# Forget gates computed inside the values' product, their block sums through DRAM, in a streaming-encoder layer

## The chip, the cores and the metric

The kernel runs on one core of a Trainium2 chip. The metric is device time in microseconds (us), from one execution to the next of the same program. TensorE (PE) does the matrix products, VectorE (DVE) and ScalarE (ACT) the elementwise work, GpSimd (POOL) a little of it, and SyncE (SP) issues every transfer.

## What is computed

One post-norm layer over a sequence of 1024 rows of width 1024: a token mixer with two branches (forgetting attention and a gated linear recurrence), then a SwiGLU feed-forward layer. The part that the change touches is the forget gate of the attention, one column of `f_a` for each of the 8 heads:

```python
proj = x @ w_in
q_a, k_a, v_a, f_a, q_b, f_b, i_b, g_b, gate_a, gate_b = jnp.split(proj, IN_SPLITS, axis=-1)
log_fa = jax.nn.log_sigmoid(f_a + b_f)              # (B, S, 8)
y_a = fox_attention(q_a, k_a, v_a, log_fa)
...
F = jnp.cumsum(log_f, axis=1).transpose(0, 2, 1)    # along the sequence
s = einsum(q_i, kh) * scale + fq_i[..., None] - F[:, :, None, :]
p = softmax(where(causal, s, -inf)); o = p @ vh
```

So no score can be finished before the running sum F of the gates' logarithms is there for its head.

## The kernel before

The whole layer is one program. Each matrix product is made with operands that are split in a high and a low part (`split`: ACT rounds to the high part, DVE subtracts it for the low part) and three matmuls for each pair. The values `v_a` and `i_b` are one product of x (1024 by 1024) with a weight (1024 by 1024), made by a recursion with seven products of half size instead of eight, p1 to p7. With x cut in quarters (x11 and x12 are the first 512 rows, x21 and x22 the last), its operands are x11 (p1), x12 (p2), x22 (p4), the sum x21 + x22 (p5), and three other sums (p6, p7, p3). The products run in the order p1, p2, p4, p5, p6, p7, p3, 48 matmuls of 512 columns each. Their names in the trace: `Tvp5h` and `Tvp5l` are the high and low part of p5's weight, `vs2`, `vs3` and `vs4` the operands of p6, p7 and p3, `vx` and `vy` the results (four PSUM banks each), `x_r` the loaded last rows of x, `vbm` the second half of the values on its way to `vb_d` in DRAM.

Then `qk_first` makes queries and keys of the first two heads with the same recursion (`qk_s`, `qk_pt`, seven products of 12 matmuls). In its middle, before queries are copied out, it calls `forget_gates`:

1. 32 matmuls, x against 8 columns of weights (`wf`, high and low part beside each other in 40 columns), give `fo` in two halves of 512 rows, and ACT and DVE add high and low results into `fs`.
2. Eight transfers turn this into one tile `f4` of 64 partitions (8 blocks of 128 rows times 8 heads), called `f` in the trace.
3. Some twelve small steps on ACT and DVE make the logarithms and a running sum along each block of 128 rows.
4. A matmul with a constant matrix `before` gives each block the sum of the blocks ahead of it, and two DVE steps add it.
5. The result goes to `nf_d` in DRAM.

`attention` handles the heads in pairs. For each head it loads `nf_d` broadcast to 128 partitions into a quarter of `box1` (`box` in the trace, 512 KB), POOL adds the causal mask to a copy of it in two steps, and for each block of 128 queries PE makes the scores `s`, DVE adds the bias and takes the maximum (`soft`), ACT takes the exponential, POOL scales, and PE transposes (`pt`) and multiplies with the values (`pv`).

All calls are first written down by a planner and then issued engine by engine in the order that its costs give (`Plan.schedule`): a call goes where its engine is free first in the plan, and among those the one that was written down earliest. The plan prices a transfer at its bytes over 358 GB/s, plus 1.95 us until it lands, and 60 ns of SP's time. The products of eight of the later gates (`gps`, weights `wg`) are written down with a rank that lets them fill what PE has free. Each engine then runs its own list strictly in order, and SP issues all transfers in one list into one queue. Tiles come out of pools with a fixed number of buffers: `box1` is in the pool of `vbm`, which has one buffer, so the first transfer into `box1` waits until all eight transfers of `vbm` to `vb_d` have been done. In the same way the weights of the second head pair (`wq_r`, 512 KB) take the buffer of a high part of `vs2`.

Of the kernel before, what the change touches and what calls it, by code (L numbers as in the profile page):

```python
# [7 lines left out]
F32 = mybir.dt.float32  # L8
# [274 lines left out]
def trunk(ctx: ExitStack, tc, a: dict, out: bass.AP):  # L283
# [52 lines left out]
    def split(hi, lo, src):  # L336
        act.copy(hi, src)
        dve.tensor_sub(lo, src, f(hi))
# [149 lines left out]

    vops["p5"] = A21
    for c in range(4):  # L490
        s1 = half("gt", f"vs1r{c}")
        dve.tensor_add(s1, a21[c], a22[c])
        split(vops["p5"][0][c], vops["p5"][1][c], s1)
    product("p5", T1, vy, True)
# [5 lines left out]
    for c in range(4):  # L500
        s3 = half("gt", f"vs3r{c}")
        dve.tensor_sub(s3, f(A11[0][c]), a21[c])
# [3 lines left out]
        split(vops["p7"][0][c], vops["p7"][1][c], s3)  # L506
    product("p6", T2, vx, True)
# [7 lines left out]
    bf = const("bf", [NT * HA, 1])  # L515
    before = const("before", [NT * HA, NT * HA + 2])
# [19 lines left out]


    wfr = const("w_f", [P, KC, HA])
    nf_d = dram.tile([NT, HA, P], F32, name="nf_d")

    def forget_gates():

        LO = 32
        wf = half("gt", "wf", F32R)[:, :KC * (LO + HA)].rearrange("p (c h) -> p c h", h=LO + HA)
        same = wfr[:, :, None, :].to_broadcast([P, KC, LO // HA - 1, HA])
        dve.tensor_sub(wf[:, :, HA:LO].rearrange("p c (a h) -> p c a h", h=HA), same, same)
        split(wf[:, :, :HA], wf[:, :, LO:], wfr)
        fs = box1[:HA, 3, :]
        for hf in range(2):
            fo = bank("h", f"fo{hf}")[:LO + HA]  # L550
            for c in range(KC):
                h, l = X(c)
                mm(fo, wf[:, c], h[:, hs(hf)], start=c == 0, stop=c == KC - 1)
                mm(fo[:HA], wf[:, c, :HA], l[:, hs(hf)], start=False, stop=c == KC - 1, skip_group_check=True)
            act.copy(fs[:, hs(hf)], fo[LO:])
            dve.tensor_add(fs[:, hs(hf)], fo[:HA], fs[:, hs(hf)])


        BH = NT * HA
        f4 = half("gt", "f4")[:BH]  # L560
        fps = f4[:, blk(1)]
        for t in range(NT):
            sync.dma_start(fps[t * HA:(t + 1) * HA], fs[:, blk(t)])
        fz, fa, fe, fu = (f4[:, blk(i)] for i in (0, 1, 2, 3))
        act.activation(fe, fps, AF.Abs, bias=bf, scale=1.0)
# [1029 lines left out]
```

## Time and profile before

| | us |
|---|---|
| median of 3 runs (lowest, highest) | 1486.25 (1485.85, 1486.31) |
| the profiled execution's own time | 1485.11 |
| its span, first to last instruction | 1483.3 |
| PE busy in the span | 1452.9 |

The page gives busy time by engine and the span in 40 slices. The views of the trace used below are: busy time by stage, with the clock that TensorE was granted (1.00 is 2.4 GHz, 0.50 is 1.2 GHz) and what the transfers moved; the timeline of one engine, where a bracket at the end of a row gives the idle time just before it and what ended it; and the rows of one tile. A row's start is counted from the first instruction of the span.

### The profile page before, as it was taken

What the parts mean: (1) busy time and instruction counts of PE and PEld (TensorE: products, weight loads), DVE (VectorE), ACT (ScalarE), POOL (GpSimd) and SP (SyncE); (2) the same over time, 40 slices, a digit from 0 to 9 for tenths busy, and PEclk for the clock granted to TensorE, in tenths of its full rate; (3) what the DMA queues carried; (4) which work ended last, traced back from release to release, by engine and by line L of the source; (5) the groups of instructions that cost most, each with busy time, mean ns of one, the idle gap of its engine ahead of it and who ended that gap; (6) DMA issues with size and microseconds to landing.
All of it is one profiled execution on the core that took longest, in us unless ns stands there. A gap on an engine that the chain in (4) does not pass through costs nothing.

```text
span 1483.3 us, 19094 instructions
## 1 busy us (share of the span) xinstructions
PE 1452.9 (98%) x6807; PEld 1193.0 (80%) x6807; DVE 1105.8 (75%) x2087; ACT 676.8 (46%) x1163; POOL 97.0 (7%) x116
## 2 busy tenths in 40 slices
PE   9997999999999999999999899999999999999998
PEld 6866888778887887788888778888888888888887
DVE  7976686776887889744838898666666666698597
ACT  6536576587576575334511343333332333434330
POOL 0003232220001000000001000000000000000000
PEclk9998999999999999999999999999999999999999
DMA  7033212221112234446720303333333335977741
GB/s 262 11 105 78 66 52 69 61 77 37 56 44 71 75 125 157 149 142 217 262 61 1 114 22 127 97 96 103 105 106 107 107 107 174 330 269 227 259 160 57
DMA packets 82208, 175.97 MB, mean 119 GB/s; under 512 B 8128, under 2 KB 21312, under 8 KB 82112
## 3 DMA queue, kind: packets, MB, share of 16 engines
q1 hardware_dynamic: 82112, 174.74, 36.2%
q8 instruction: 54, 0.88, 0.2%
q14 instruction: 42, 0.34, 0.1%
HBM read 135.58 MB, written 39.09 MB: 118 GB/s over the span
## 4 chain that ended last, share of the span: by engine, by line
PE 87%; DVE 6%; DMA 4%; issue 1%; ACT 1%; SPq 1%; POOL 1%; DVEq 0%; POOLq 0%; ACTq 0%
PE p L279 14%; PE fb L279 11%; PE fc L279 8%; PE fa L279 8%; PE bps L279 7%; PE pps L279 6%; PE o L279 6%; PE gs L279 5%; PE gps L279 3%; PE pv L279 2%; PE kps L279 2%; PE vx L279 2%; PE s L279 2%; PE pt L279 2%; PE qps L279 2%; PE vy L279 1%
## 5 line engine op out<-in xcount | busy, mean ns | idle before, releaser
L279 PE MATMUL p<-dp 128*128 128x512 f32 (+1 forms) x957 | 210.0, 382 | 0.0
L279 PEld LDWEIGHTS p<-dp 128*128 128x128 f32 x957 | 175.4, 188 | 34.7
L279 PE MATMUL fc<-xs,Tp 128*128 128x512 f32 x528 | 127.1, 389 | 0.0
L279 PE MATMUL fb<-xs,Tp 128*128 128x512 f32 x528 | 126.7, 389 | 0.0
L279 PE MATMUL fa<-x,Tp 128*128 128x512 f32 x480 | 115.7, 389 | 0.3 <-DVE u L279 0.3
L279 PEld LDWEIGHTS fc<-xs,Tp 128*128 128x128 f32 x528 | 99.1, 188 | 20.7 <-ACT xs L279 0.2
L279 PEld LDWEIGHTS fb<-xs,Tp 128*128 128x128 f32 x528 | 99.2, 188 | 20.6
L279 ACT CAST Tp<-t 128x512 fp32r<-128x512 f32 x88 | 54.3, 620 | 116.5 <-PE fc L279 71.9
L279 DVE TENSOR_TENSOR Tp<-t,Tp 128x512 fp32r<-128x512 f32 x88 | 60.6, 690 | 60.5 <-ACT Tp L279 60.1
L279 PEld LDWEIGHTS fa<-x,Tp 128*128 128x128 f32 x480 | 90.1, 188 | 19.3 <-ACT p L279 0.7
L279 ACT CAST dp<-dap 128x1024 fp32r<-128x1024 f32 (+1 forms) x42 | 41.1, 982 | 95.6 <-PE p L279 48.8
L279 PE MATMUL bps<-xl,wb_h 128*128 128x512 f32 x192 | 76.0, 396 | 0.0
L279 PE MATMUL bps<-xh,wb_h 128*128 128x512 f32 x192 | 76.0, 396 | 0.0
L279 PE MATMUL bps<-xh,wb_l 128*128 128x512 f32 x192 | 75.7, 396 | 0.0
L279 POOL TENSOR_TENSOR norm<-norm,mhalf 128x1 f32<-128x1 f32 x16 | 14.6, 914 | 882.5 <-DVE norm L279 882.5
L279 DVE TENSOR_TENSOR tl<-pt,th 128x512 fp32r<-128x512 f32 (+1 forms) x96 | 50.6, 552 | 16.5 <-ACT th L279 15.9
L279 ACT ACTIVATE p<-p,soft 128x128 f32<-128x128 f32 (+3 forms) x64 | 49.5, 775 | 22.4 <-DVE soft L279 22.0
L279 DVE TENSOR_TENSOR dp<-dap,dp 128x1024 fp32r<-128x1024 f32 (+1 forms) x42 | 47.4, 1129 | 14.9 <-ACT dp L279 14.9
L279 PE MATMUL fb<-x,Tp 128*128 128x512 f32 x240 | 57.7, 389 | 0.0
L279 POOL TENSOR_SCALAR p<-p,soft 128x128 f32<-128x128 f32 (+3 forms) x64 | 47.5, 750 | 110.8 <-DVE soft L279 97.7
L279 ACT CAST th<-pt 128x512 fp32r<-128x512 f32 (+1 forms) x96 | 43.1, 477 | 23.6 <-PE pt L279 22.2
L279 ACT CAST Tp<-wg_r 128x512 fp32r<-128x512 f32 x40 | 24.9, 623 | 62.0 <-PE fb L279 32.2
(512 smaller groups left out, 3523.4 us busy)
## 6 DMA issues: line engine op xcount, KB each, us to landing
dbp<-in_w_fo SPq DMA_DIRECT2D x45, 512.0 KB
dap<-a_d SPq DMA_DIRECT2D x35, 512.0 KB
a_d<-ar SPq DMA_DIRECT2D x42, 256.0 KB
wu_r<-in_w_ff SPq DMA_DIRECT2D x20, 512.0 KB
wg_r<-in_w_ff SPq DMA_DIRECT2D x20, 512.0 KB
a_d<-as SPq DMA_DIRECT2D x33, 256.0 KB
wg_r<-in_w_g SPq DMA_DIRECT2D x16, 512.0 KB
sg<-gate_d SPq DMA_DIRECT2D x32, 256.0 KB
```

Source lines behind the costliest of these rows:

```text
L279: getattr(q.engine, method)(*args, **kw)
```

## The change

The function `forget_gates` moves up into the values' products, between the sums for p5 and the product p5. It multiplies operands that are there already. For the first half of the rows these are x11 and x12 with the weights w1 and w2, as before. For the second half they are x21 + x22 and x22, with w1 and w2 - w1, which gives x21 w1 + x22 w2. The differences stand behind the weights in `wfx` (12 instead of 8 groups of columns). The results go into two of the banks `vx`, which p4 has left.

What was eight transfers between tiles is now two to DRAM (`f_d`) and one back. The matmul for the sums of the blocks is replaced: the last column of the running sums goes to DRAM (`b_d`, 64 numbers), eight transfers bring it back (8 partitions of 8 numbers each), and DVE multiplies by a mask and adds along the row. The four tiles `vs3r` are gone: x21's raw copy is overwritten with the difference, and loaded again from DRAM afterwards for `qk_first`.

```diff
--- before.py
+++ after.py
@@ -486,11 +486,73 @@
     for t in range(4):
         act.copy(va[:, 4 + t, :], vx[t])
 
+
+    nf_d = dram.tile([NT, HA, P], F32, name="nf_d")
+
+    def forget_gates():
+
+        LO, NC = 32, KC + 4
+        wfx = keep([P, NC, HA], "wfx")
+        sync.dma_start(wfx[:, :KC], a["w_f"])
+        dve.tensor_sub(wfx[:, KC:], wfx[:, 4:KC], wfx[:, :4])
+        wf = half("gt", "wf", F32R)[:, :NC * (LO + HA)].rearrange("p (c h) -> p c h", h=LO + HA)
+        same = wfx[:, :, None, :].to_broadcast([P, NC, LO // HA - 1, HA])
+        dve.tensor_sub(wf[:, :, HA:LO].rearrange("p c (a h) -> p c a h", h=HA), same, same)
+        split(wf[:, :, :HA], wf[:, :, LO:], wfx)
+        f_d = dram.tile([NT, HA, P], F32, name="f_d")
+        for hf, ops in enumerate(((A11, A12), (vops["p5"], A22))):
+            fo = vx[1 + hf][:LO + HA]
+            for c in range(KC):
+                h, l = (x[c % 4] for x in ops[c // 4])
+                w = wf[:, c + 4 * (hf and c > 3)]
+                mm(fo, w, h, start=c == 0, stop=c == KC - 1)
+                mm(fo[:HA], w[:, :HA], l, start=False, stop=c == KC - 1, skip_group_check=True)
+            fs = half("gt", f"fs{hf}")[:HA]
+            act.copy(fs, fo[LO:])
+            dve.tensor_add(fs, fo[:HA], fs)
+            sync.dma_start(f_d[4 * hf:4 * hf + 4].rearrange("t h p -> h t p"), fs.rearrange("h (t p) -> h t p", p=P))
+
+
+        BH = NT * HA
+        f4 = half("gt", "f4")[:BH]
+        fz, fa, fe, fu = (f4[:, blk(i)] for i in range(4))
+        sync.dma_start(fa, f_d.rearrange("t h p -> (t h) p"))
+        act.activation(fe, fa, AF.Abs, bias=bf, scale=1.0)
+        dve.tensor_scalar(fa, fa, bf, 0.0, op0=ALU.add, op1=ALU.min)
+        act.activation(fe, fe, AF.Exp, scale=-1.0)
+        dve.tensor_scalar(fu, fe, 1.0, None, op0=ALU.add)
+        act.activation(fz, fu, AF.Ln)
+        dve.tensor_scalar(fu, fu, -1.0, None, op0=ALU.add)
+        dve.tensor_sub(fe, fe, fu)
+        act.activation(fu, fz, AF.Exp, scale=-1.0)
+        dve.tensor_mul(fe, fe, fu)
+        dve.tensor_add(fz, fz, fe)
+        nf = fe
+        dve.tensor_tensor_scan(nf, fz, fa, 0.0, op0=ALU.add, op1=ALU.subtract)
+
+
+        b_d = dram.tile([NT, HA], F32, name="b_d")
+        sync.dma_start(b_d.rearrange("t h -> (t h)").unsqueeze(1), nf[:, P - 1:P])
+        dve.tensor_sub(fz, fz, fa)
+        bs = fa[:, :NT]
+        for t in range(NT):
+            sync.dma_start(bs[t * HA:(t + 1) * HA], b_d.rearrange("t h -> h t"))
+        dve.tensor_mul(bs, bs, before[:, :NT])
+        base = fu[:, :1]
+        dve.tensor_reduce(base, bs, axis=mybir.AxisListType.X, op=ALU.add)
+        dve.tensor_scalar(fz, fz, before[:, NT + 1:NT + 2], base, op0=ALU.mult, op1=ALU.add)
+        dve.scalar_tensor_tensor(nf, nf, before[:, NT:NT + 1], fz, op0=ALU.mult, op1=ALU.add)
+        sync.dma_start(nf_d.rearrange("t h p -> (t h) p"), nf)
+
+    bf = const("bf", [NT * HA, 1])
+    before = const("before", [NT * HA, NT + 2])
+
     vops["p5"] = A21
     for c in range(4):
         s1 = half("gt", f"vs1r{c}")
         dve.tensor_add(s1, a21[c], a22[c])
         split(vops["p5"][0][c], vops["p5"][1][c], s1)
+    forget_gates()
     product("p5", T1, vy, True)
     vbm = take("m", [NT, NB], "vbm")
     for t in range(4):
@@ -498,12 +560,13 @@
     vops["p6"] = operand4(("wr0", "wr1", "pf", "pf"), "vs2")
     vops["p7"] = operand4(("qk", "qk", "pf", "pf"), "vs3")
     for c in range(4):
-        s3 = half("gt", f"vs3r{c}")
-        dve.tensor_sub(s3, f(A11[0][c]), a21[c])
+        s3 = a21[c]
+        dve.tensor_sub(s3, f(A11[0][c]), s3)
         dve.tensor_add(s3, s3, f(A11[1][c]))
         dve.tensor_sub(a22[c], a22[c], s3)
         split(vops["p6"][0][c], vops["p6"][1][c], a22[c])
         split(vops["p7"][0][c], vops["p7"][1][c], s3)
+        sync.dma_start(s3, a["xT"][c][:, hs(1)])
     product("p6", T2, vx, True)
     for t in range(4):
         dve.tensor_add(vbm[:, t, :], vx[t], p1v[t])
@@ -512,8 +575,6 @@
     product("p7", T3, vx, False)
     ident = const("ident", [P, P])
     causal = const("causal", [P, 2, P], BF16, "mask")
-    bf = const("bf", [NT * HA, 1])
-    before = const("before", [NT * HA, NT * HA + 2])
 
     vops["p3"] = operand4(("kb", "kb", "qk", "qk"), "vs4")
     for c in range(4):
@@ -535,55 +596,6 @@
         sync.dma_start(vb_d[t], vbm[:, t, :])
 
 
-    wfr = const("w_f", [P, KC, HA])
-    nf_d = dram.tile([NT, HA, P], F32, name="nf_d")
-
-    def forget_gates():
-
...
-        fs = box1[:HA, 3, :]
-        for hf in range(2):
-            fo = bank("h", f"fo{hf}")[:LO + HA]
-            for c in range(KC):
-                h, l = X(c)
-                mm(fo, wf[:, c], h[:, hs(hf)], start=c == 0, stop=c == KC - 1)
-                mm(fo[:HA], wf[:, c, :HA], l[:, hs(hf)], start=False, stop=c == KC - 1, skip_group_check=True)
-            act.copy(fs[:, hs(hf)], fo[LO:])
-            dve.tensor_add(fs[:, hs(hf)], fo[:HA], fs[:, hs(hf)])
-
-
-        BH = NT * HA
-        f4 = half("gt", "f4")[:BH]
-        fps = f4[:, blk(1)]
-        for t in range(NT):
-            sync.dma_start(fps[t * HA:(t + 1) * HA], fs[:, blk(t)])
-        fz, fa, fe, fu = (f4[:, blk(i)] for i in (0, 1, 2, 3))
...
-        base = bank("h", "fbase")[:BH, :1]
-        mm(base, before[:, :BH], nf[:, P - 1:P], start=True, stop=True)
-        dve.tensor_sub(fz, fz, fa)
-        dve.tensor_scalar(fz, fz, before[:, BH + 1:BH + 2], base, op0=ALU.mult, op1=ALU.add)
-        dve.scalar_tensor_tensor(nf, nf, before[:, BH:BH + 1], fz, op0=ALU.mult, op1=ALU.add)
-        sync.dma_start(nf_d.rearrange("t h p -> (t h) p"), nf)
-
-
     ya_d = dram.tile([4, P, S], F32, name="ya_d")
 
     def qk_tiles(p):
@@ -641,7 +653,6 @@
         act.copy(p1, oa)
         mul("p2", b21, oa, False)
         dve.tensor_sub(t2, b22, b12)
-        forget_gates()
         qk_heads(0, 0, oa, *tiles)
         mul("p6", t2, ob, True)
         dve.tensor_add(u2, ob, p1)
@@ -1514,11 +1525,11 @@
         nw = 64 // L
         for c in range(2):
             lmask[:, c, nw - 1:2 * nw - 1] = (s[:, None] // (2 * L) == np.arange(nw)) & (s[:, None] // L % 2 == c)
-    bh = np.arange(NT * HA)
-    t, h = bh // HA, bh % HA
-    before = np.zeros((NT * HA, NT * HA + 2), np.float32)
-    before[:, :-2] = (h[:, None] == h) & ((t[:, None] < t) | (t[:, None] == t) & (t % 2 == 1))
-    before[:, -2], before[:, -1] = 1 - 2 * (t % 2), t % 2
+    t = np.arange(NT * HA)[:, None] // HA
+    b = np.arange(NT)
+    before = np.zeros((NT * HA, NT + 2), np.float32)
+    before[:, :-2] = (b < t) | (b == t) & (t % 2 == 1)
+    before[:, -2:] = np.concatenate([1 - 2 * (t % 2), t % 2], axis=1)
     return {"before": before, "ident": ident, "causal": causal, "once": once,
             "lmask": lmask}
 
```

How the lists of the engines read at three places follows; in each, the first block is the kernel before and the second the changed one.

SP, from the transfers of `vbm` to the loads that the first head pair waits for (`f_213<-box_179` and `f_128<-b_d` are the two forms of the small loads, `box<-nf_d` the bias of one head each, the `wq_r` behind `vb_d` the weights of the second head pair; those of the first pair, `wq_r` and `wk_r`, show in the second block only):

```order
L279 DMA vb_d<-vbm 128x512 x8
L279 DMA f_213<-box_179 8x128 x8
L279 DMA wq_r<-in_w_qk 128x1024
L279 DMA wg_0_r<-in_w_g 128x1024
L279 DMA nf_d<-f_213 64x128
L279 DMA box_179<-nf_d 128x8x128 x2
L279 DMA wg_1_r<-in_w_g 128x1024
L279 DMA wk_r<-in_w_qk 128x1024
```

```order
L279 DMA f_128<-b_d 8x8x1 x8
L279 DMA nf_d<-f_128 64x128
L279 DMA wq_r<-in_w_qk 128x1024
L279 DMA wk_r<-in_w_qk 128x1024
L279 DMA vb_d<-vbm 128x512 x8
L279 DMA box_181<-nf_d 128x8x128 x2
L279 DMA wq_r<-in_w_qk 128x1024
L279 DMA wg_0_r<-in_w_g 128x1024
```

Before, the second pair's `wq_r` stands ahead of the two bias loads; now it stands behind them, and they follow the transfers of `vbm` at once.

ACT, ahead of the copies of the keys (`k`, `kl`) that the first scores read:

```order
L279 COPY box_179<-fo_211 8x512
L279 COPY box_179<-fo_212 8x512
L279 ACTIVATE f_213<-f_213,bf 64x128
L279 ACTIVATE f_213<-f_213 64x128 x2
L279 CAST wq_h_368<-wq_r 128x512
L279 ACTIVATE f_213<-f_213 64x128
L279 CAST k_0_0_200<-qk_u_193 64x512 x2
L279 CAST k_0_1_201<-qk_u_193 64x512 x2
```

```order
L279 ACTIVATE q_0_1_201<-qk_s 64x512
L279 CAST wq_h_365<-wq_r 128x512
L279 CAST k_0_0_202<-qk_u_195 64x512 x2
L279 CAST k_0_1_203<-qk_u_195 64x512
L279 CAST kl_0_204<-kl_0_204 64x512
L279 CAST k_0_1_203<-qk_u_195 64x512
L279 CAST kl_1_205<-kl_1_205 64x512
L279 CAST k_0_0_202<-qk_p_196 64x512 x2
```

The steps on `f` are gone from there, and the cast of `wq_r` stands ahead of the first copy of the keys in both.

DVE, at the end of p7's operands and the beginning of p3's (`vs4l`):

```order
L279 TENSOR_TENSOR Tvp7l_156<-b_1_81,Tvp7h_152 128x512
L279 TENSOR_TENSOR x_r<-xh_67,x_r 128x512
L279 TENSOR_TENSOR vbm<-vx_74,p1v_106 128x512
L279 TENSOR_TENSOR x_r<-x_r,xl_69 128x512
L279 TENSOR_TENSOR x_r<-xh_67,x_r 128x512 x2
L279 TENSOR_TENSOR vs4l_163<-x_r,vs4h_161 128x512
L279 TENSOR_TENSOR x_r<-x_r,xl_69 128x512 x2
L279 TENSOR_TENSOR x_r<-xh_67,x_r 128x512
L279 TENSOR_TENSOR vs4l_163<-x_r,vs4h_161 128x512
```

```order
L279 TENSOR_TENSOR x_r<-xh_67,x_r 128x512
L279 TENSOR_TENSOR vbm<-vx_72,p1v_105 128x512
L279 TENSOR_TENSOR x_r<-x_r,xl_69 128x512
L279 TENSOR_TENSOR x_r<-xh_67,x_r 128x512
L279 TENSOR_TENSOR f_128<-f_128,before 64x8
L279 TENSOR_TENSOR x_r<-xh_67,x_r 128x512
L279 TENSOR_REDUCE f_128<-f_128 64x1
L279 TENSOR_TENSOR vbm<-vx_73,p1v_106 128x512
L279 TENSOR_SCALAR f_128<-f_128,before 64x128
L279 TENSOR_TENSOR vs4l_167<-x_r,vs4h_165 128x512
L279 SCALAR_TENSOR_TENSOR f_128<-f_128,before 64x128
```

The last steps of the gates' chain stand between the steps for `vs4`; the first of them reads what the eight small loads bring.

## Rows read from the trace of the kernel before

**Rows 1.** The page, busy time of the engines: us, share, instructions

```profile
PE 1452.9 (98%) x6807; PEld 1193.0 (80%) x6807; DVE 1105.8 (75%) x2087; ACT 676.8 (46%) x1163; POOL 97.0 (7%) x116
```

**Rows 2.** Busy time by stage: stretch, length, engines, clock, transfers' share, GB/s

```profile
33.00:100.00 67.00, 67.00 (x295) 52.38 (x294) 64.55 (x112) 33.03 (x58) 0.00 (x0) 1.00 0.14 49
...
122.00:128.00 6.00, 0.98 (x5) 0.48 (x3) 0.32 (x3) 0.00 (x0) 1.50 (x2) 0.82 0.69 122
128.00:136.00 8.00, 6.33 (x21) 4.83 (x22) 3.80 (x25) 2.98 (x9) 3.89 (x6) 0.71 0.45 169
```

**Rows 3.** PE's timeline around the attention's start: start, us, engine, line, operation

```profile
108.77 0.39 PE L279 MATMUL qk_pt<-vs3h,Tqkp7l 128*128 128x512 f32 x1
110.86 0.50 PE L279 MATMUL s<-k,q 128*128 128x128 f32 x2 [1.71 <-ACT k L279]
...
122.59 0.39 PE L279 MATMUL gps<-xh,wg_l 128*128 128x512 f32 x1
128.13 0.77 PE L279 MATMUL s<-k,q 128*128 128x512 f32 x1 [5.14 <-DVE soft L279]
...
134.44 0.33 PE L279 MATMUL pt<-ident,p 128*128 128x128 f32 x1 [1.55 <-POOL p L279]
```

**Rows 4.** The gates' chain on DVE, SP and POOL: timelines of these engines

```profile
111.31 0.41 DVE L279 TENSOR_TENSOR_SCAN f<-f 64x128 f32<-64x128 f32 x1
114.02 0.51 SPq L279 DMA_DIRECT2D nf_d<-f  x1
117.11 1.02 SPq L279 DMA_DIRECT2D box<-nf_d  x2
126.50 2.27 POOL L279 TENSOR_TENSOR box<-box,causal 128x512 f32<-128x512 f32 x2 [126.06 <-DMA box<-nf_d]
132.87 1.15 POOL L279 TENSOR_TENSOR box<-box,causal 128x512 f32<-128x512 f32 x1 [4.11 <-DMA box<-nf_d]
```

**Rows 5.** The gates' tile `fo`: its matmuls with a high part

```profile
L279 PE MATMUL fo<-xh,wf x16: 387/397/403, 90.6 to 100.3; 128*40 128x512 f32 x16
```

**Rows 6.** PE's first matmuls of p7 and p3, DVE's last steps for p3

```profile
63.41 0.39 PE L279 MATMUL vx<-Tvp7h,vs3h 128*128 128x512 f32 x1
74.29 0.39 PE L279 MATMUL vy<-Tvp3h,vs4h 128*128 128x512 f32 x1
72.09 1.30 DVE L279 TENSOR_TENSOR Tvp3l<-b,Tvp3h 128x512 fp32r<-128x512 f32 x2
73.29 1.29 DVE L279 TENSOR_TENSOR p1v<-vx,p1v 128x512 f32<-128x512 f32 x2
```

**Rows 7.** Small transfers and what waited for them: SP's and ACT's timelines

```profile
102.31 2.64 SPq L279 DMA_DIRECT2D f<-box  x4
106.21 0.40 ACT L279 ACTIVATE f<-f,bf 64x128 f32<-64x128 f32 x1 [4.64 <-DMA f<-box]
24.42 3.76 SPq L279 DMA_DIRECT2D x_r<-in_xT  x8
71.05 1.28 ACT L278 ACT_TABLE_LOAD   x1
```

**Rows 8.** The second pair's weights on SP, then ACT's copies behind their cast

```profile
105.06 0.37 SPq L279 DMA_DIRECT2D wq_r<-in_w_qk  x1
108.83 0.62 ACT L279 CAST wq_h<-wq_r 128x512 fp32r<-128x512 f32 x1 [1.28 <-DMA wq_r<-in_w_qk]
116.99 0.61 ACT L279 CAST kl<-kl 64x512 fp32r<-64x512 f32 x1
118.30 1.29 ACT L279 ACTIVATE q<-qk_p 64x512 fp32r<-64x512 f32 x2
```

**Rows 9.** The load issued behind the bias loads (SP); transfers by stage

```profile
118.99 2.82 SPq L279 DMA_DIRECT2D wg_r<-in_w_g  x1
118.00:125.00 7.00, 4.98 (x22) 3.78 (x21) 3.02 (x5) 2.12 (x4) 0.00 (x0) 1.00 0.79 72
126.00:133.00 7.00, 4.76 (x12) 3.55 (x12) 2.54 (x18) 2.98 (x9) 2.39 (x3) 0.52 0.47 167
```

More of the change, by code (lines that the diff above doesn't have):

```diff
@@ L535, in trunk @@
         sync.dma_start(vb_d[t], vbm[:, t, :])
-    wfr = const("w_f", [P, KC, HA])
-    nf_d = dram.tile([NT, HA, P], F32, name="nf_d")
-    def forget_gates():
[L543 to L547, printed above, removed]
-        fs = box1[:HA, 3, :]
-        for hf in range(2):
-            fo = bank("h", f"fo{hf}")[:LO + HA]
-            for c in range(KC):
-                h, l = X(c)
-                mm(fo, wf[:, c], h[:, hs(hf)], start=c == 0, stop=c == KC - 1)
-                mm(fo[:HA], wf[:, c, :HA], l[:, hs(hf)], start=False, stop=c == KC - 1, skip_group_check=True)
-            act.copy(fs[:, hs(hf)], fo[LO:])
-            dve.tensor_add(fs[:, hs(hf)], fo[:HA], fs[:, hs(hf)])
-        BH = NT * HA
-        f4 = half("gt", "f4")[:BH]
-        fps = f4[:, blk(1)]
-        for t in range(NT):
-            sync.dma_start(fps[t * HA:(t + 1) * HA], fs[:, blk(t)])
-        fz, fa, fe, fu = (f4[:, blk(i)] for i in (0, 1, 2, 3))
-        act.activation(fe, fps, AF.Abs, bias=bf, scale=1.0)
-        dve.tensor_scalar(fa, fps, bf, 0.0, op0=ALU.add, op1=ALU.min)
-        act.activation(fe, fe, AF.Exp, scale=-1.0)
-        dve.tensor_scalar(fu, fe, 1.0, None, op0=ALU.add)
-        act.activation(fz, fu, AF.Ln)
-        dve.tensor_scalar(fu, fu, -1.0, None, op0=ALU.add)
-        dve.tensor_sub(fe, fe, fu)
-        act.activation(fu, fz, AF.Exp, scale=-1.0)
-        dve.tensor_mul(fe, fe, fu)
-        dve.tensor_add(fz, fz, fe)
-        nf = fe
-        dve.tensor_tensor_scan(nf, fz, fa, 0.0, op0=ALU.add, op1=ALU.subtract)
-        base = bank("h", "fbase")[:BH, :1]
-        mm(base, before[:, :BH], nf[:, P - 1:P], start=True, stop=True)
-        dve.tensor_sub(fz, fz, fa)
-        dve.tensor_scalar(fz, fz, before[:, BH + 1:BH + 2], base, op0=ALU.mult, op1=ALU.add)
-        dve.scalar_tensor_tensor(nf, nf, before[:, BH:BH + 1], fz, op0=ALU.mult, op1=ALU.add)
-        sync.dma_start(nf_d.rearrange("t h p -> (t h) p"), nf)
     ya_d = dram.tile([4, P, S], F32, name="ya_d")
```

## The prediction

> **What bounds the kernel.** I read the page first: PE is busy for 1452.9 us of a span of 1483.3 [rows 1], so some 30 us are open to any change that leaves PE's work alone, as this one does. Busy time by stage then tells where. From 33 to 100 us PE has no idle time at all, and DVE is busy for 64.55 of these 67 us [rows 2]: the values' stage is full on both engines, and that is where the work goes. From 122 to 128 us PE does 0.98 us of work, and from 128 to 136 it runs at a mean clock of 0.71 [rows 2]: that is the hole. PE's timeline names its parts: 1.71 us of waiting for the copies of the keys before the first score, 5.14 us for a bias step on DVE, and 1.55 us for POOL before the first transpose [rows 3]. The last two come from the gates' chain, and the other engines show it: the running sum ends at 111.7, its write is issued at 114.02, the two bias loads follow at 117.11, and POOL can start on the first head at 126.50 and on the second at 132.87 [rows 4]. So the hole is a chain that starts too late, and its longest links are the bias loads: 126.5 - 117.1 = 9.4 us for the first head, 15.8 for both.
>
> **The matmuls** move as they are: 32 before and after. Of 512 columns each, they cost what p7's do: 48 from 63.41 to 74.29, 0.227 us each [rows 6]; the tile of the gates shows the same 0.39 us from start to end as any of these [rows 5]. So PE comes 32 x 0.227 = 7.3 us later to p3 and the same amount sooner out of the queries' products: zero in sum. For the small matmul over the blocks I carry nothing.
>
> **DVE's steps** move too. A step of 512 columns takes 0.60 us (two from 72.09 to 73.29 [rows 6]); ahead of p3's last operand there come two such steps and some 15 small ones, none above the 0.41 us of the running sum [rows 4] and most near half of it, together about 5 us. Before, DVE finishes p3's operands at 73.3 and PE wants the last of them ten matmuls behind 74.29, at 76.5 [rows 6]: 3.2 us to spare. With PE 7.3 us later, DVE may still stand and wait for 3.2 + 7.3 - 5 = 5.5 us before PE has to wait with it. Covered, if the next term stays below that.
>
> **The chain's transfers.** PE ends the gates' matmuls near 50.4 (p5 starts two products of 10.9 before 63.41, with six matmuls ahead of the 32), and ACT and DVE add 1.3. A transfer that the next one waits for takes 3.1 us on a write to DRAM (114.02 to 117.11 [rows 4]) and about 1.9 on a small load: four of them go out in 2.64 us from 102.31, so the last near 104.3, and ACT starts at 106.21 [rows 7]. The tile `f4` is there at 51.8 + 3.1 + 1.9 = 56.8. From there to the end of the running sum it was 106.21 to 111.72 before [rows 4, 7], 5.5 us; the load of the activation table, 1.28 us and hidden before [rows 7], now stands in it: 63.6. Then the write of the block sums, 3.1, and eight loads. Their spacing is 0.47 us by the large loads and 0.66 by the small ones [rows 7], so the last goes out 3.3 to 4.6 us after the first, and 1.9 more: 71.9 to 73.2. I take 73.2, from the small ones. DVE comes to the step that reads them after eight steps of 0.60 and two small ones, near 69. It stands for about 4 us, and everything on its list stands behind it. That is below 5.5, so p3 costs nothing, with some 1.3 us in hand.
>
> **The bias loads.** They need the buffer of `vbm`, whose last transfer waits for DVE: from 73.2 the list has 35 steps of 512 columns and 1.5 us of small ones, 22.5 us, so 95.7. A transfer to DRAM is worth 1.9 to 3.1; at 2.5 the bias loads go out at 98.2, 19 us sooner than at 117.11. By the same 9.4 and 15.8 us they are there at 107.6 and 114.0. The first scores are not due before 110, so the waits of 5.14 and 1.55 us and the slow stretch behind them are gone as far as the bias is their cause. That alone would be worth some 8 us.
>
> **What is late next.** The weights `wq_r` of the second head pair. Before, they go out at 105.06, ahead of the bias loads, and ACT, whose list has their cast ahead of the keys' copies, starts it at 108.83 after 1.28 us of waiting: 3.8 us from issue, and the first score comes 2.0 us later at 110.86 [rows 3, 8]. Now they stand behind two bias loads in the one queue, at about 104, when PE has left the buffer. Not below 104 + 3.8 = 107.8, then; 108.5 leaves room for the later PE. Upward, the load issued behind the two bias loads before is the row to read: SP needs 2.82 us for it instead of 0.37 [rows 8, 9]. From 118 to 125 us the transfers move 72 GB/s, 0.50 MB, one bias load and nothing else; from 126 to 133 they move 1.17 MB, the second bias load (0.52) and 0.65 of what stands behind [rows 9]. So that load of 0.52 MB ended between 131 and about 134, 14 to 17 us after the first bias load went out. I take 15.7: 98.2 + 15.7 = 113.9 for the cast of `wq_r`, 5 us later than before.
>
> The Trainium skill says of this, in DMA: Bandwidth & Descriptors, section Queues, rings and completion order, that each transfer engine consumes the descriptors of a queue in the order of its ring. The 0.65 MB that passed while the second bias load was still under way show that not all engines are at the same place, so the trace agrees for one engine at most. Taken for whole transfers it would put `wq_r` behind the second load, at 98.2 + 15.8 + 1 = 115.0, and the time 1.1 us higher; it is counted in the upper part of my range.
>
> **From the cast on.** ACT's list runs from it through the keys' copies, three exponentials, two copies of queries and the cast of the gate weights that PE needs after its first three transposes. Before, cast to last key copy was 108.83 to 117.6 with some 1.4 us of other work and waits in between, so 7.4; the two query copies took 1.29 [rows 8]; with three exponentials and the cast I estimate 11.4 in all. PE goes on at 113.9 + 11.4 = 125.3. In the kernel before, the same place (three transposes done, at about 135.1, 0.65 after the row at 134.44 [rows 3]) has 28 gate matmuls and the first scores of two more query blocks behind it that the changed one still has to do: 7.4 us, so 127.7. Gain 2.4. PE now idles about 6 us in one piece before the first score, and the clock was down for a while after 5.14 [rows 2, 3]; I take off 0.6 for a second, shorter wait. Forecast: 1.8 us gained, 1485.11 - 1.8 = 1483.3 against the profiled execution, whose 1.8 us outside the span stay; on the median, 1486.25 - 1.8 = **1484.5**.
>
> **Rivals.** *The weights slip past* (0.24). If `wq_r` lands as soon as after any other issue, at 108.5, all that hangs on the cast comes 5.4 us sooner: 1479.1. For it: 0.65 MB passed a bias load. Against: nothing did in the first 7 us [rows 9].
> *The block sums come late* (0.13), the slower side. Every microsecond by which the eight loads land later moves the bias loads and the cast by as much. No row shows a transfer of 4-byte pieces; if each of the two trips takes 2.5 us longer than taken here, the loads land at 78.2, the gain of 1.8 becomes a loss of 3.2, and PE waits at p3 as well, inside the same loss: 1489.5. It decides from a landing near 78, that is from about 9 us of waiting on DVE.
> *The sums come early* (0.11): loads there by 70, DVE hardly waits, the last transfer of `vbm` is then set by PE's p3, and the cast comes at 112: 1482.5.
> The forecast itself (0.52) reaches from 1482.5 to 1487.5, by the 14 to 17 us.
>
> **The numbers.** A measurement of this kernel can tell about 0.2%, 3.0 us, from no change: bounds 1483.3 and 1489.2. Faster: the first rival, most of the third and a small part of the forecast, 0.24 + 0.09 + 0.04 = 0.37. Slower: the second rival in its worse part and a little for what I overlook, 0.13. Same: 0.50. The range that leaves out 2 in 10 goes from 1478.8 to 1489.0.
>
> **What would show it.** Right: PE without idle time from 33 us to the end of p7 of the queries; DVE's wait on the block sums of 3 to 5 us near 70; bias loads issued near 98; PE's idle time before the first score 5 to 6 us, released by ACT's key copies, with ACT in turn waiting for `wq_r`; no wait on the bias. Wrong, if ACT waits for `wq_r` under 2 us (first rival), if p3 has idle time on PE (second), or if PE loses time behind 140 us, where the lists differ up to 260 and I have priced nothing.

## The result, and the profile after

The changed kernel takes 1488.55 us (median of 14 runs) against 1486.05 of the kernel before (14 runs): the ratio is 1.0018, with a 95% interval of 1.0010 to 1.0027. It is 2.7 us slower, where 1.8 us of gain were forecast. The profiled execution has a span of 1486.6 us, 3.3 more than before.

TensorE has the same work as in [rows 1], spread differently. The page's line of busy times, and then busy time by stage (us and count for each engine, granted clock, share of the transfer engines' time, GB/s):

```profile
PE 1455.0 (98%) x6805; PEld 1191.1 (80%) x6805; DVE 1107.8 (75%) x2090; ACT 677.6 (46%) x1163; POOL 99.1 (7%) x116
```

```profile
33.00:75.00 42.00, 42.00 (x186) 31.68 (x184) 33.89 (x64) 21.64 (x40) 0.00 (x0) 1.00 0.10 28
75.00:78.00 3.00, 1.09 (x5) 0.67 (x4) 2.25 (x7) 0.00 (x0) 0.00 (x0) 1.00 0.00 0
...
113.00:118.00 5.00, 0.30 (x2) 0.00 (x0) 0.35 (x1) 1.00 (x2) 2.26 (x2) 0.92 0.48 164
118.00:124.00 6.00, 5.00 (x13) 3.92 (x14) 4.70 (x12) 5.80 (x11) 0.00 (x0) 0.50 0.00 0
124.00:129.00 5.00, 3.52 (x16) 2.43 (x15) 3.79 (x14) 4.74 (x12) 1.47 (x3) 1.00 0.00 0
```

The old hole of 122 to 128 us [rows 2] is gone. A new one stands from 113 to 118 us, with half the clock for 6 us behind it, and a small one at 75 to 78. PE's timeline of the changed kernel names both; the rows answer to [rows 3]:

```profile
77.24 0.50 PE L279 MATMUL vx<-Tvp7h,vs3h 128*128 128x512 f32 x1 [1.91 <-DVE vbm L279]
...
118.84 1.12 PE L279 MATMUL s<-k,q 128*128 128x128 f32 x3 [5.53 <-ACT k L279]
...
126.59 0.35 PE L279 MATMUL s<-k,q 128*128 128x256 f32 x1 [0.59 <-DVE soft L279]
128.02 0.44 PE L279 MATMUL pt<-ident,p 128*128 128x128 f32 x2 [0.55 <-POOL p L279]
128.71 0.50 PE L279 MATMUL gps<-xh,wg_h 128*128 128x512 f32 x1 [0.26 <-ACT wg_h L279]
```

The waits that came from the bias (5.14 us for DVE's `soft` and 1.55 for POOL's `p` before) are down to 0.59 and 0.55, and the bias itself is there by then: POOL starts on it at 110.05 and 115.73. In their place the first score waits 5.53 us for the copies of the keys. ACT shows why: the cast of the second pair's query weights, ahead of them on its list, waits for its load.

```profile
117.00 0.62 ACT L279 CAST wq_h<-wq_r 128x512 fp32r<-128x512 f32 x1 [8.37 <-DMA wq_r<-in_w_qk]
```

How late that load is was decided 40 us earlier. SP's queue and DVE of the changed kernel:

```profile
61.92 0.47 SPq L279 DMA_DIRECT2D b_d<-f  x1
68.28 2.73 SPq L279 DMA_DIRECT2D f<-b_d  x8
78.33 0.47 SPq L279 DMA_DIRECT2D nf_d<-f  x1
...
87.95 11.55 SPq L279 DMA_DIRECT2D vb_d<-vbm  x8
101.40 1.00 SPq L279 DMA_DIRECT2D box<-nf_d  x2
106.48 0.35 SPq L279 DMA_DIRECT2D wq_r<-in_w_qk  x1
```

```profile
66.21 0.68 DVE L279 TENSOR_TENSOR x_r<-xh,x_r 128x512 f32<-128x512 f32 x1
75.75 0.16 DVE L279 TENSOR_TENSOR f<-f,before 64x8 f32<-64x8 f32 x1 [8.86 <-DMA f<-b_d]
...
76.51 0.67 DVE L279 TENSOR_TENSOR vbm<-vx,p1v 128x512 f32<-128x512 f32 x1
```

The write of the 64 block sums goes out at 61.92, the loads that wait for it only 6.36 us later, and DVE's step on them starts 7.47 us after that, having stood for 8.86 us. Behind it on DVE's list stand the steps that fill `vbm`, but for the first two: the transfers of `vbm` go out late, the bias loads with them (101.40), the query weights behind those.

### The profile page after: what moved, and what is told of

Its sections match the earlier page's. It is cut to its first block, busy times and chain, and to the rows that moved or that the text cites. A ratio compares the mean times of both kernels' runs of the same rounds, so it can differ in the third digit from the quotient of the medians.

```text
span 1486.6 us, 19086 instructions
## 1 busy us (share of the span) xinstructions
PE 1455.0 (98%) x6805; PEld 1191.1 (80%) x6805; DVE 1107.8 (75%) x2090; ACT 677.6 (46%) x1163; POOL 99.1 (7%) x116
## 4 chain that ended last, share of the span: by engine, by line
PE 84%; DVE 9%; DMA 4%; issue 1%; ACT 1%; SPq 1%; POOL 1%; DVEq 0%; ACTq 0%; POOLq 0%
PE p L279 14%; PE fb L279 11%; PE fa L279 8%; PE fc L279 8%; PE bps L279 8%; PE pps L279 6%; PE o L279 6%; PE gs L279 5%; PE gps L279 4%; PE pv L279 2%; PE kps L279 2%; PE s L279 2%; PE pt L279 2%; PE qps L279 2%; DMA b<-in_w_v 1%; PE lp L279 1%
## 5 line engine op out<-in xcount | busy, mean ns | idle before, releaser
L279 POOL TENSOR_SCALAR p<-p,soft 128x384 f32<-128x384 f32 (+4 forms) x64 | 49.1, 772 | 130.2 <-DVE soft L279 113.4
L279 ACT ACTIVATE p<-p,soft 128x384 f32<-128x384 f32 (+4 forms) x64 | 49.6, 777 | 13.2 <-DVE soft L279 12.9
```

Source lines behind the costliest of these rows:

```text
L279: getattr(q.engine, method)(*args, **kw)
```

## The experiments

Three theories. **A**: the trip of the block sums through DRAM is too long, and all that follows on DVE and in the queue moves with it, one to one. **B**: TensorE's loss is the place of the query weights, behind two bias loads and ahead of the keys' copies, whatever DVE does. **R**: the loss comes from the reloads of x, the fuller values' stage, or from work behind 130 us. The table has the runs that share TensorE's order with the changed kernel (with the matmul of the sums, one more). "Write" is from the issue of `b_d` to that of the first load, "loads" from there to DVE's step, the next four columns are the starts of the bias loads' issue, of the cast of `wq_r`, the distance between them, and the start of the first score.

| kernel | write | loads | bias | cast | apart | score | ratio to before (95%) |
|---|---|---|---|---|---|---|---|
| changed | 6.36 | 7.47 | 101.40 | 117.00 | 15.60 | 118.84 | 1.0018 (1.0010 to 1.0027) |
| without the trip | - | 8.54 | 98.96 | 114.49 | 15.53 | 116.32 | 0.9998 (0.9989 to 1.0007) |
| 32-byte loads | 7.41 | 4.03 | 99.05 | 114.59 | 15.54 | 116.42 | 1.0000 (0.9991 to 1.0009) |
| sums by matmul | - | - | 95.49 | 110.27 | 14.78 | 112.10 | 0.9973 (0.9961 to 0.9984) |
| trip told to the planner | 6.45 | 8.82 | 94.34 | 109.94 | 15.60 | 111.76 | 0.9971 (0.9956 to 0.9985) |
| whole rows written | 1.84 | 4.29 | 94.68 | 110.37 | 15.69 | 112.20 | 0.9966 (0.9953 to 0.9978) |
| 4-byte pieces, apart | 1.71 | 4.24 | 94.94 | 111.04 | 16.10 | 112.87 | 0.9972 (0.9962 to 0.9982) |
| bias from ACT's queue | 7.12 | 7.43 | 104.47 | 119.83 | 15.36 | 121.67 | 1.0022 (1.0012 to 1.0031) |
| the same, whole rows | 1.84 | 4.31 | 95.04 | 110.75 | 15.71 | 112.58 | 0.9971 (0.9960 to 0.9983) |

### Loads that wait for nothing (1484.99 us)

```diff
-            sync.dma_start(bs[t * HA:(t + 1) * HA], b_d.rearrange("t h -> h t"))
+            sync.dma_start(bs[t * HA:(t + 1) * HA], a["bf"].rearrange("(t h) o -> h (t o)", h=HA))
```

> The eight loads of block sums read a constant input of the same shape in place of the 64 sums that the kernel has just written to DRAM (so the block offsets of the bias, and with them the output, are left out); the write of the sums stays, nobody reads it. Everything else, the loads' place in the queue too, is the changed kernel's. Theory A: the trip of the 4-byte pieces (write issued 61.92, loads only from 68.28 on, DVE standing 8.86 us for them until 75.75) is the fault: it holds the sum that p7's banks wait for (1.91 us of TensorE), and it shifts vb_d, the bias loads (issued 101.40) and with them the query weights' copy (117.00) by about 3 us. Then DVE's wait falls under 1 us, p7's wait goes, the bias loads are issued at 97 to 99, the query weights are copied at 113 to 114.5, and the time is 2.5 to 4 us under the changed kernel's 1488.5: 1484.5 to 1486. Theory B: the query weights stand behind the two bias loads in the queue whatever DVE does, and what TensorE loses there (5.53 us at 118.84) is set by that order alone: the copy then comes earlier by as much as the bias loads do, but TensorE waits just as long, and the time falls by 0 to 2 us. Rival R: the changed kernel loses its time in the reloads of x and the longer values' stage or after 130 us: no change, 1488 to 1489.

The wait of p7 went, the bias loads came 2.4 us sooner and the time fell by 3 us, as A has it. (One thing moved that the expectation does not name: the planner, for which the loads now wait for no write, puts DVE's step two places earlier on its list.) But DVE still stood for 5.56 us: 4-byte loads out of 256 bytes take long here too, where the kernel has written nothing. The eight took 5.98 us to go out, against 2.73 in the changed kernel:

```profile
63.61 5.98 SPq L279 DMA_DIRECT2D f<-in_bf  x8
```

```profile
72.15 0.16 DVE L279 TENSOR_TENSOR f<-f,before 64x8 f32<-64x8 f32 x1 [5.56 <-DMA f<-in_bf]
```

TensorE's wait before the first score stayed at 5.30 us, and the time fell nevertheless, since all of it came sooner. R cannot account for these 3 us: nothing in the reloads or behind 130 us was touched.

### The block sums by a matmul (1481.20 us)

```diff
-        b_d = dram.tile([NT, HA], F32, name="b_d")
-        sync.dma_start(b_d.rearrange("t h -> (t h)").unsqueeze(1), nf[:, P - 1:P])
+        base = bank("h", "fbase")[:BH, :1]
+        mm(base, before[:, :BH], nf[:, P - 1:P], start=True, stop=True)
```

(The loads, the mask and the row sum go as well, and the constant `before` has its old form.)

> The block sums by one matmul into a bank as in the kernel before, in the changed kernel's place; no trip through DRAM for them, all else as changed. Theory A: as without the trip: DVE's wait of 8.86 us is gone, p7 loses no time, the bias loads are issued at 97 to 99, the time is 1484.5 to 1486. A cost of the matmul of its own: TensorE may stand for the running sum at the place where the matmul is put among p7's, which would be seen as a wait on DVE's f there. Rival R: no change against 1488.5.

Better than expected. DVE does not stand at all, the bias loads go out 5.9 us sooner, and the time is 6.7 us under the changed kernel. No wait of PE's on the running sum shows.

### The planner told of the trip (1481.43 us)

```diff
-                lat = self.OWN[q] if uq == q else self.LAT[q]
+                lat = (self.OWN[q] if uq == q else self.LAT[q]) + self.extra[i]
...
+        plan.lag = 4400.0
         sync.dma_start(b_d.rearrange("t h -> (t h)").unsqueeze(1), nf[:, P - 1:P])
...
+        plan.lag = 5400.0
         for t in range(NT):
             sync.dma_start(bs[t * HA:(t + 1) * HA], b_d.rearrange("t h -> h t"))
```

(`extra` holds the value of `lag` at each step; it is set back to 0 behind each of the two places.)

> The changed kernel with one number told to the planner: the 4-byte write and the eight 4-byte loads take 4.4 and 5.4 us longer than its 1.95 us, as the trace has them. The trip stays as it is; DVE takes its other work first and comes to the block sums last. Theory A: the loss is in DVE standing, not in the trip itself: DVE's wait falls from 8.86 us to under 1, p7's 1.91 goes, but nf_d is written later, between the parts of vb_d, so the bias loads are issued at 98 to 100; 1484.5 to 1486.5. If the trip itself decides (the mask's write as the last thing ahead of the bias loads), the bias loads stay at 101 or later and the time at 1487 to 1489. Rival R: no change, 1488 to 1489.

The trip is no shorter (6.45 us for the write, 8.82 from the first load to DVE's step), and it costs hardly anything. DVE comes to it with other work done first, and stands for 0.68 us:

```profile
77.05 0.16 DVE L279 TENSOR_TENSOR f<-f,before 64x8 f32<-64x8 f32 x1 [0.68 <-DMA f<-b_d]
```

The step itself is later than in the changed kernel (75.75), the bias loads go out 7.1 us sooner, and the time falls by 7.0 us. So it is DVE standing, not the lateness of the sums, that moves what follows. This is A in its sharper form.

### The planner told of the spread loads (1481.73 us)

```diff
-        return float(o.nbytes()) / 358.0
+        return float(o.nbytes()) / (62.0 if any(x.ap[0][0] == 0 and x.ap[0][1] == P for x in ins) else 358.0)
```

> The changed kernel with one other number told to the planner: a load that spreads one row over all partitions moves 62 GB/s and not 358, which makes each bias load 8.5 us of its own queue as the trace has it, so that ACT copies the query weights after the keys' copies and not ahead of them. The trip and DVE's wait stay. The number also reorders later work, of the other heads. Theory B: TensorE's wait of 5.53 us at 118.84 is the price of that place in ACT's order: it goes, the scores of the first head start some 5 us earlier, and the time falls by 3 to 5.5 us to 1483 to 1485.5, with p7's 1.91 us still there. Theory A alone: the scores start earlier but wait for the biases in DVE instead (bias issue 101.40, landing 110 and 116), and the time moves by less than 1.5 us. Rival R: no change.

The 5.53 us are gone, as B had it, and p7 still waits (2.54 us at 78.70). But waits on the scores' own chain come in: 4.6 us in three, the largest two

```profile
121.31 0.35 PE L279 MATMUL s<-k,q 128*128 128x256 f32 x1 [1.35 <-DVE soft L279]
...
125.37 0.66 PE L279 MATMUL s<-k,q 128*128 128x384 f32 x1 [2.63 <-DVE soft L279]
```

The ratio is 0.9977 (0.9967 to 0.9988), 6.1 us under the changed kernel. That is more than B's place on ACT's list explains, given those new waits. By the pages, PE is idle 2.9 us less and busy 3.1 us less for the same 6805 matmuls (1451.9 us in a span of 1480.6, against 1455.0 in 1486.6); where the second part comes from is open. The run with the kernel before, below, says what else the number does.

### Both numbers (1476.75 us), and the matmul with the second (1476.98 us)

The edits are the two above together, and the matmul with the spread loads' price.

> The changed kernel with both numbers told to the planner: the longer trip of the 4-byte pieces, and 62 GB/s for a load that spreads one row over all partitions. Each alone gave 3.6 to 3.9 us under the kernel before, 6 to 6.4 under the changed one. If they are two causes, with TensorE's remaining wait on the keys' copies (3.0 us with the longer trip alone) as what is left for the second: that wait goes and the time comes to 7 to 9.5 us under the changed kernel, 1476 to 1479 against 1485.3 to 1486 for the kernel before. If they are one cause (each only makes the query weights' copy come in time): no more than either alone, 1481 to 1482.5.

> The block sums by a matmul as in the kernel before, and 62 GB/s told to the planner for the spread loads. With the matmul alone 1481.2, a wait of 2.5 us on the keys' copies left. Two causes: the wait goes, 1477 to 1479.5. One cause: 1480.5 to 1482. A cost of its own that speaks against it: scores that start earlier wait for DVE's bias steps, as in the run with the spread loads' price alone, where TensorE lost 4.6 us in three such waits; then 1480 to 1482 with those waits in the trace.

Ratios 0.9945 (0.9932 to 0.9957) and 0.9949 (0.9936 to 0.9961): two causes, which add up for the most part (each alone 3.4 to 4.3 us under the kernel before, both 7.6 to 8.2). The wait on the keys' copies is gone in both (0.21 us is left in the first), the waits on DVE's steps are as in the run with the price alone (4.5 and 4.6 us).

### Loads of 32 bytes (1485.35 us)

```diff
-            sync.dma_start(bs[t * HA:(t + 1) * HA], b_d.rearrange("t h -> h t"))
+            sync.dma_start(bs[t * HA:(t + 1) * HA], b_d)
```

> Each of the eight loads brings the 8 by 8 block sums as they lie in DRAM, 32 bytes to a partition, and not transposed in 64 pieces of 4 bytes (so the sums over blocks are wrong, and the output with them); the write, the order on every engine and the number of transfers are the changed kernel's. If the size of the pieces sets what the loads take (7.47 us from the first's issue at 68.28 to DVE's step at 75.75): 4 to 5.5 us, DVE goes on at 72.5 to 74, and the time falls by 1.5 to 3 us against 1488.5. If the number of transfers or the trip of each does: 7 to 8 us as before and the time unchanged, 1488 to 1489.

```profile
69.56 2.66 SPq L279 DMA_DIRECT2D f<-b_d  x8
```

```profile
73.59 0.16 DVE L279 TENSOR_TENSOR f<-f,before 64x8 f32<-64x8 f32 x1 [6.48 <-DMA f<-b_d]
```

The number of transfers does not decide: 4.03 us against 7.47 for the same eight. Whether it is the size of the piece or its placing, the next two runs tell. The time falls by 2.7 us against the changed kernel; p7 does not wait, though DVE stands for 6.48 us.

### Whole rows written (1479.06 us)

```diff
-        b_d = dram.tile([NT, HA], F32, name="b_d")
-        sync.dma_start(b_d.rearrange("t h -> (t h)").unsqueeze(1), nf[:, P - 1:P])
+        b_d = dram.tile([NT, HA, P], F32, name="b_d")
+        sync.dma_start(b_d.rearrange("t h p -> (t h) p"), nf)
...
-            sync.dma_start(bs[t * HA:(t + 1) * HA], b_d.rearrange("t h -> h t"))
+            sync.dma_start(bs[t * HA:(t + 1) * HA], b_d[:, :, P - 1].rearrange("t h -> h t"))
```

> The running sum is written to DRAM as whole rows of 512 bytes, 64 of them, in place of its last column as 64 pieces of 4 bytes; the eight loads then pick their 4-byte pieces out of the rows. The result is the same, and so is the order on every engine. If the 4-byte write is what takes the 6.36 us from its issue to the loads' issue: 2 to 3.2 us (as the write of nf_d or of f_d before its load), DVE goes on 3 to 4 us sooner, at 71.5 to 73, and the time falls by 2.5 to 3.5 us against 1488.5, as without the trip. If any write that a load waits for takes so long here: 6 to 6.5 us and no change.

128 times the bytes, and 4.5 us less; the loads, 4-byte pieces still, gained 3.2 us as well, which no theory had. SP's queue of this kernel, DVE and ACT:

```profile
62.12 0.47 SPq L279 DMA_DIRECT2D b_d<-f  x1
63.96 2.74 SPq L279 DMA_DIRECT2D f<-b_d  x8
```

```profile
68.25 0.16 DVE L279 TENSOR_TENSOR f<-f,before 64x8 f32<-64x8 f32 x1 [1.17 <-DMA f<-b_d]
```

```profile
110.37 0.62 ACT L279 CAST wq_h<-wq_r 128x512 fp32r<-128x512 f32 x1 [6.89 <-DMA wq_r<-in_w_qk]
```

With the order on every engine unchanged, this run is A's plainest proof: DVE's step 7.5 us sooner, the cast 6.6, the time 7.7 (by the ratios).

### 4-byte pieces, 512 bytes apart (1481.12 us)

```diff
-        sync.dma_start(b_d.rearrange("t h p -> (t h) p"), nf)
+        sync.dma_start(b_d.rearrange("t h p -> (t h) p")[:, P - 1:P], nf[:, P - 1:P])
```

(against whole rows)

> The 64 sums are written as 64 pieces of 4 bytes, as in the changed kernel, but 512 bytes apart in DRAM and not side by side in 256 bytes; the eight loads pick them up there. Same result, same order on every engine, same number of transfers and bytes as the changed kernel. If it is the side-by-side placing that makes the write slow: its trip takes 1.8 to 2.2 us as with whole rows (6.36 in the changed kernel), DVE stands 1 to 1.5 us, and the time is 6 to 7 us under the kernel before. If it is the size of the piece: 6 to 7 us for the write, then 4.3 us for the loads as with whole rows (7.47 when they lie side by side), DVE goes on near 72.5 to 73.5, and the time is 0 to 1.5 us under the kernel before, as with the loads of 32-byte pieces.

```profile
62.38 0.47 SPq L279 DMA_DIRECT2D b_d<-f  x1
64.09 2.73 SPq L279 DMA_DIRECT2D f<-b_d  x8
```

```profile
68.33 0.16 DVE L279 TENSOR_TENSOR f<-f,before 64x8 f32<-64x8 f32 x1 [0.99 <-DMA f<-b_d]
```

The placing decides, not the size: the same 64 pieces of 4 bytes take 1.71 us to the next issue where they lie 512 bytes apart, and 6.36 side by side. The same holds for the loads, 4.24 against 7.47. The trace's transfer records say where the write loses its time: in both kernels all its 80 packets are started within 0.2 us, 1.1 us after the issue, and in the changed kernel no other packet starts from then until the loads are issued at 68.28. So the time goes by behind the start of the last packet, before the write is reported done, and not in sending. What in the chip makes neighbours slow the runs do not show. The time is 4.2 us under the kernel before by the ratio, less than the 6 to 7 expected from the run with whole rows; that run itself is 5.0 under by its ratio, and the two intervals overlap.

### The bias loads from ACT's queue (1487.39 us), and with whole rows (1480.17 us)

```diff
+            plan.lag = 8000.0
-            sync.dma_start(nfx[:, :, 1, :], nf_d[:, h, :].partition_broadcast(P))
+            act.dma_start(nfx[:, :, 1, :], nf_d[:, h, :].partition_broadcast(P))
+            plan.lag = 0.0
```

(The planner prices such an issue at 100 ns of ACT.)

> The changed kernel with the bias loads issued from ACT's queue in place of SP's; TensorE and DVE have the same order as in the changed kernel, the trip and DVE's wait of 8.86 us stay. Theory B1, the order in the one queue: the query weights no longer stand behind the two bias loads; they land 2.5 to 4 us after their issue at 106.5, ACT copies them by 111 or sooner, TensorE's wait of 5.53 us on the keys' copies falls under 1 us, and the gate weights are ready some 5 us sooner; the time is 1482 to 1485. Theory B2, the transfer engines themselves: they are shared, whichever queue a load is in, and the copy of the query weights stays at 114 to 117; 1487 to 1490. A cost of its own: ACT may stand for the buffer of the values at the place of the issue, up to 1 us.

> Whole rows for the running sum's write, and the bias loads from ACT's queue. If the order in the one queue holds the query weights back (theory B1), the 3.9 us of waiting on the keys' copies that whole rows alone left go as well: 1474.5 to 1477. If the transfer engines do (B2): 1478.5 to 1480.

B1 falls. In another queue than the bias loads, the query weights come no sooner. ACT's timeline of the first of the two:

```profile
104.47 1.02 ACTq L279 DMA_DIRECT2D box<-nf_d  x2
...
119.83 0.62 ACT L279 CAST wq_h<-wq_r 128x512 fp32r<-128x512 f32 x1 [8.15 <-DMA wq_r<-in_w_qk]
```

15.36 us from the bias issue to the cast, 15.71 with whole rows; 14.8 to 16.1 where all three stand in SP's queue. So what holds the weights lies behind the queues, in what both share, for about 15 us with two spread loads of 0.52 MB. The Trainium skill has this in DMA: Bandwidth & Descriptors, section Issuing engines are not separate DMA queues: transfers started by different engines end up on the same 16 transfer engines and interleave there. The trace agrees: from 113 to 118 us of the first run 157 packets of SP's queue (0.58 MB, the weights) and 445 of ACT's (0.22 MB, the second bias load) move side by side. That the engines are full then is not shown: they are busy for 59% of these 5 us.

### Whole rows and the price (1477.41 us), and the kernel before with the price (1478.18 us)

The edits are those above; in the second, the price alone, on the kernel before.

> The running sum written as whole rows, and 62 GB/s told to the planner for the spread loads. Whole rows alone gave 1479.1 with a wait of 3.9 us left on the keys' copies; the price took that wait away in two other kernels, and put 4.5 us of waits on DVE's steps in its place, with a net gain of 4.5 us. The same net gain here would be 1474.5 to 1477; if the two only overlap, 1478 to 1480.

> The kernel before with 62 GB/s told to the planner for the spread loads, nothing else. In it the query weights go out ahead of the bias loads, and ACT waits for them 1.28 us only. If the price helps by the place of the query weights' copy alone, there is little to win: 1484 to 1487, with the waits on the bias (5.14 and 1.55 us) as they were. If it helps by other moves (the later heads), the kernel before gains as well: 1480 to 1483.

Ratios 0.9949 (0.9936 to 0.9961) and 0.9950 (0.9937 to 0.9964). The first time lies between its two expectations. Whole rows and the price come to what the planner's two numbers gave together (0.9945), so the shorter trip is one cause with DVE's standing. The second run went past both expectations: the kernel before, with one number of its planner corrected and its gates where they were, is as fast as the best of the changed ones within the intervals. Its rows for the stretches of [rows 2] say how:

```profile
122.00:128.00 6.00, 6.00 (x28) 4.99 (x27) 0.51 (x4) 0.59 (x1) 1.42 (x2) 1.00 0.49 120
128.00:136.00 8.00, 6.93 (x36) 5.17 (x35) 6.81 (x43) 5.21 (x15) 3.80 (x7) 1.00 0.44 169
```

The bias comes as late as ever (POOL starts on it at 126.58). But a planner that knows this puts the gate products ahead of the scores that wait for it, and TensorE is busy for 6.00 of the 6 us in which it did 0.98 before. From 115 to 140 us it is idle for 1.91 us instead of 6.69, which is 4.8 of the 5.5 us by which the profiled span is shorter (1477.8 us). So the price helps by more than the query weights' place, and the hole that the change was made around could be filled without moving the gates.

## Why the prediction was wrong

The forecast was 1484.5 and the kernel takes 1488.55, inside the range (1478.8 to 1489.0) but on the other side of the kernel before. By its own steps:

- **The matmuls move for zero**: right for the 32. PE is busy for all of the 42 us from 33 to 75.
- **DVE may stand for 5.5 us before PE has to wait**: the size was near, the place wrong. I looked at p3's operands. The first to wait is p7, which adds into the banks `vx`: DVE's sums into `vbm` read them first and stand behind the block sums on its list. Where p7 waits, DVE's wait less PE's is the same each time: 8.86 - 1.91 = 6.95, 9.50 - 2.54 = 6.96 (price alone), 9.59 - 2.63 = 6.96 (bias from ACT's queue). So DVE may stand 6.95 us, and at 6.48 (32-byte loads) p7 indeed does not wait.
- **The chain up to the running sum**: right, a little early (61.9, forecast 63.6).
- **The block sums' trip**: the term that failed. I took 3.1 us for the write, from the write of 64 rows of 512 bytes, and 6.5 from the first load to the last one's landing, by issue spacings and 1.9 us. They took 6.36 and 7.47, so the step on DVE comes at 75.75 instead of 73.2, with the running sum 1.7 us ahead of the forecast. I had said that no row shows 4-byte pieces and had the right consequence as a rival (0.13), with the two trips 2.5 us longer each. The write was 3.3 longer, the loads 1.0, and that the loads are only 1.0 out is luck: they go out in 2.73 us instead of about 5, but DVE's step comes 4.74 us after the end of their issue where I had put 1.9 for the last one.
- **From the block sums to the bias loads**: 22.5 and 2.5 us forecast, 25.65 measured from 75.75 to 101.40. The loads go out 3.2 us later than forecast, 2.55 of it from the term above.
- **The bias there at 107.6 and 114.0**: POOL starts at 110.05 and 115.73, that is 8.65 and 14.3 us after the issue instead of 9.4 and 15.8. Their waits are gone as forecast.
- **The cast of the query weights 15.7 us after the bias loads' issue**: 15.60. Right, and what I took from two windows of [rows 9] held in nine kernels to within a microsecond. The order of a ring, which I had put beside it from the Trainium skill (DMA: Bandwidth & Descriptors, section Queues, rings and completion order), is not what sets it: with the bias loads in another queue the weights came no sooner.
- **From the cast to the gate weights' matmuls 11.4 us**: 11.71. So these start at 128.71 and not at 125.3, 3.4 us late, and 3.2 of it is the late issue of the bias loads.
- **The same place of the kernel before at 127.7**: by this the changed one loses 1.0 us there, and 1.6 with the clock as I carried it. At the first product of `dg`, 370 us into the span, it is 2.4 us behind. The 0.8 us between I can't place; 0.4 is idle time of PE between 200 and 300 us. The profiled span's other microsecond (3.3 in all) falls where the change touches nothing: the first matmuls of `fa`, at the start of the feed-forward layer, take 11.62 us before (843.17 to 854.79) and 12.75 after (845.32 to 858.07), at mean granted clocks of 0.87 and 0.77.
- **The rivals.** "The block sums come late" is what happened, at 75.75 and not at 78, and turned the sign there already: a forecast gain of 1.8 us is used up by a bias issue 3.2 us late. "The sums come early" is what whole rows and pieces set apart give: loads there by 70, cast forecast at 112, measured 110.4 and 111.0, time forecast 1482.5, measured 1479.1 and 1481.1. "The weights slip past" happened in none of the nine kernels of the table.

What I did not price at all: the planner's list could also have been made right. The planner takes each spread load for 1.5 us (0.52 MB at its 358 GB/s), and it takes one trip of the block sums for 1.95 us. Both numbers are behind the two waits.

## What to carry to other kernels

When a short chain through DRAM stands in the middle of a busy engine's list, price it by who is queued behind the step that waits, and tell the planner its real length: the same trip cost 7 us more with DVE standing 8.86 us for it than with the step put later and DVE standing 0.68. Where a term has no row, the forecast should not rest on the cheaper neighbour: 4-byte pieces were priced by the row for 512-byte rows, and that one choice turned the sign. Before moving work out of a hole, ask whether the planner would fill the hole itself if it knew how long the awaited transfer takes.

## What the runs showed of the hardware that I had not expected

- **64 numbers side by side in DRAM are slow, 64 numbers set apart are not.** Written with 4 bytes to a piece, next to each other in 256 bytes: 6.36 to 7.41 us to the issue that waits. 512 bytes apart: 1.71. As whole rows with 128 times the bytes: 1.84. Read in 4-byte pieces side by side: 7.15 to 8.8 us for eight transfers in the runs where DVE waits for them; 4.2 to 4.3 set apart, 4.03 in 32-byte pieces. The Trainium skill has in DMA: Bandwidth & Descriptors, section Specifications, that transfers below 512 bytes are done by reading, changing and writing back. The size alone cost the write nothing here (1.71 us against 1.84).
- **Two loads that each spread one row over all partitions hold back the load behind them**, also when that is in another queue: with 0.52 MB each, 14.8 to 16.1 us from their issue to the use of the next load.
- **Waits of nearly one length met different clocks.** With whole rows TensorE waited 3.95 us, and with pieces set apart 4.33 us, at the same place and with the same order; the first ran at 0.66 and then at full clock, the second at 0.50 and 0.91 (first whole rows, then pieces apart; the clock is the third number from the end):

```profile
113.00:118.00 5.00, 4.51 (x14) 3.70 (x15) 3.58 (x11) 4.88 (x9) 0.00 (x0) 0.66 0.00 0
118.00:124.00 6.00, 4.50 (x21) 3.08 (x20) 5.55 (x19) 5.49 (x14) 1.85 (x3) 1.00 0.01 3
```

```profile
113.00:118.00 5.00, 4.84 (x13) 3.77 (x14) 3.71 (x11) 4.86 (x9) 0.00 (x0) 0.50 0.00 0
118.00:124.00 6.00, 4.54 (x18) 2.85 (x18) 4.28 (x16) 5.25 (x13) 1.84 (x3) 0.91 0.00 0
```

The first gate matmul then starts at 121.76 and 123.22: 1.5 us apart, for 0.7 between the two first scores. The length of the wait does not order this: from the first score to the first gate matmul it is 9.56 and 10.35 us in these two, 9.67 after a wait of 5.19 us (bias from ACT's queue) and 10.77 after one of 3.02 (trip told to the planner), with TensorE's list the same in all four.
